# A decoder layer on one core: the third piece of the start moved from SyncE's queue to ScalarE's, and an eighth warming matmul

## The chip, the core and the metric

The kernel runs on one core of a Trainium2 chip. The metric is the device time of one execution in microseconds (us); smaller is better. TensorE (PE) does the matrix products, VectorE (DVE) and ScalarE (ACT) convert operands and evacuate results, GpSimd (POOL) builds masks and loads small parameters, SyncE (SP) issues nearly all transfers. ACT can issue transfers too, on a DMA queue of its own. PE's clock has two levels, 1.2 and 2.4 GHz; the share of the higher one that was granted stands in the profile.

## The reference, cut to what matters

One layer on 256 tokens of width 1024: a SwiGLU channel mixer, a token mixer of three attention branches merged by gates, and a second SwiGLU, each followed by a residual sum and a LayerNorm.

```
D_MODEL, SEQ, D_FF = 1024, 256, 2816

def swiglu(x, w_gate, w_up, w_down):
    return (jax.nn.silu(x @ w_gate) * (x @ w_up)) @ w_down

x = layer_norm(alpha * x + 0.5 * swiglu(x, ffn_w_gate[l, 0], ffn_w_up[l, 0], ffn_w_down[l, 0]), ...)
x = layer_norm(alpha * x + hybrid_mixer(x, w_in[l], ...), ...)
x = layer_norm(alpha * x + 0.5 * swiglu(x, ffn_w_gate[l, 1], ffn_w_up[l, 1], ffn_w_down[l, 1]), ...)
```

Only the first few microseconds of the first `x @ w_gate` and `x @ w_up` matter here. All data are float32.

## The kernel before

Every float32 operand is split into a high part (a copy rounded to the matmul's type, made by ACT or DVE) and a low part (the operand minus its high part, made by DVE). A product is then three matmuls: high times high, low times high, high times low. One helper, `Pe.mm`, records all of them, so that they all stand on line 182.

The contraction over 1024 runs in KT = 8 tiles of 128 rows, called k = 0 to 7. For the start the host lays out an array `start`: for each k a piece of 128 rows by 768 numbers, of which 256 are the transposed activations and 512 are weight columns (the first two column blocks of gate and up). The piece of k is loaded into the tile `sraw{k}` (393,216 bytes, the 384 KB of the trace). SP issues them in order of k on its queue, except that the second half of k = 0 goes on ACT's queue. SP then goes on with the weight chunks `raw<-gu` (line 80) on the same queue.

While these are on the way, PE runs WARM matmuls on a tile of zeros, `warm`, into a bank that is not read. Then, for k = 0, 1, 2, ..., the pieces are split (lines 268 to 277 for k below 3, lines 236 and 237 in the helper `act_split` for the rest), and for each k six matmuls of 512 columns follow: high times high for two halves of the tokens, then activations' low times weights' high, then activations' high times weights' low. The lines are written in order of k for each engine, and each engine works its list in that order. For k = 1 and 2 DVE makes the activations' high part (line 274) and ACT the weights' (line 275). For k from 3 on ACT makes both, activations first.

After the eight k tiles PE goes on to the column blocks 2 to 21 of gate and up, whose weights come as the chunks of line 80, then to the down projection, the mixer and the second SwiGLU. The last work is the LayerNorm of the second half of the tokens and its transfer out.

Of the kernel before, what the change touches and what calls it, by code (L numbers as in the profile page):

```python
# [12 lines left out]
AF = mybir.ActivationFunctionType  # L13
# [19 lines left out]
HL_BUFS = 9  # L33
RAW_BUFS = 5
START = 4
WARM = 7

NAT = 2

# [151 lines left out]
def trunk(ctx: ExitStack, tc: tile.TileContext, start_d, x_d, ln_g, ln_b, gu_d, gun_d, down_d, v_d, qk_d, gate_d,  # L191
          b_gate, lam_d, subln_d, br_d, wo_d, out_d):
    nc = tc.nc
# [41 lines left out]
    def act_split(dst_h, dst_l, src):  # L235
        nc.scalar.activation(dst_h, src, AF.Copy)  # L236
        nc.vector.tensor_tensor(dst_l, src, dst_h.bitcast(F32), op=ALU.subtract)


    with ExitStack() as es:  # L240
        st = es.enter_context(tc.tile_pool(name="start", bufs=1))
        raws = []
        for k in range(KT):
            r = st.tile([P, S + 512], F32, name=f"sraw{k}")
            if k == 0:
                nc.sync.dma_start(out=r[:, 0:384], in_=start_d[k][:, 0:384])  # L246
                nc.scalar.dma_start(out=r[:, 384:768], in_=start_d[k][:, 384:768])
            else:
                nc.sync.dma_start(out=r, in_=start_d[k])  # L249
            raws.append(r)  # L250
        warm = st.tile([P, P], F32, name="warm")
        nc.vector.memset(warm, 0.0)
        wps = att.tile([P, 512], F32, name="att")

        for _ in range(WARM):
            nc.tensor.matmul(wps[:, 0:P], lhsT=warm, rhs=warm, start=True, stop=True)
        ident = const.tile([P, P], F32, name="ident")
        make_identity(nc, ident)
        first = []
        for k in range(KT):  # L260
            if k % 2 == 0:
                w = W.tile(-1 - k)
                first.append(w)
            c = slice((k % 2) * 512, (k % 2) * 512 + 512)
            rx, rw = raws[k][:, 0:S], raws[k][:, S:S + 512]
            if k == 0:

                nc.scalar.activation(xT[:, 0, 0:S], rx, AF.Copy)
                nc.vector.tensor_copy(w[:, 0, 0:P], rw[:, 0:P])
                nc.vector.tensor_copy(w[:, 0, P:512], rw[:, P:512])  # L270
                nc.vector.tensor_tensor(xT[:, 0, S:2 * S], rx, xT[:, 0, 0:S].bitcast(F32), op=ALU.subtract)
                nc.vector.tensor_tensor(w[:, 1, c], rw, w[:, 0, c].bitcast(F32), op=ALU.subtract)
            elif k < 3:
                nc.vector.tensor_copy(xT[:, k, 0:S], rx)
                nc.scalar.activation(w[:, 0, c], rw, AF.Copy)  # L275
                nc.vector.tensor_tensor(xT[:, k, S:2 * S], rx, xT[:, k, 0:S].bitcast(F32), op=ALU.subtract)
                nc.vector.tensor_tensor(w[:, 1, c], rw, w[:, 0, c].bitcast(F32), op=ALU.subtract)
            else:
                act_split(xT[:, k, 0:S], xT[:, k, S:2 * S], rx)
                act_split(w[:, 0, c], w[:, 1, c], rw)  # L280
        W.pump()
# [692 lines left out]
```

## Time and profile before

| | us |
|---|---|
| median of 3 runs | 599.16 (598.97 to 599.27) |
| the profiled execution, its time | 598.51 |
| its span, first to last instruction | 596.8 |
| PE busy in the span | 587.8 |
| DVE busy | 407.5 |
| ACT busy | 328.2 |
| mean granted clock of PE | 0.995 |

The profiled execution's time is its span and 1.71 us around it; it lies 0.65 us under the median of the runs. The busy time of PE is modelled at the ends of matmuls, since they are pipelined: a matmul's end lies behind the start of the next one.

### The profile page before, as it was taken

Reading aid. Unit: us, or ns where it says so; the run is one execution under the profiler, and the core shown is the slowest. Engines: PE = TensorE matmul, PEld = TensorE weight load, DVE = VectorE, ACT = ScalarE, POOL = GpSimd, SP = SyncE. Lnnn points to the kernel's source line nnn. Section 1 sums busy time; section 2 is a strip of 40 time slices with the busy share of each in tenths; the row PEclk is TensorE's granted clock in tenths of the full one; section 3 lists DMA queues with packets and bytes.
Section 4 is the critical chain, followed back from the end, with each engine's and each line's share of the span. In section 5 each row is a group of like instructions: output and inputs, shape, how many; then the busy total and the mean of one; then the engine's idle time right before and its main releaser. Section 6 shows DMA issues by size and latency. Waiting matters only on the chain.

```text
span 596.8 us, 8546 instructions
## 1 busy us (share of the span) xinstructions
PE 587.8 (98%) x3150; PEld 505.2 (85%) x3150; DVE 407.5 (68%) x655; ACT 328.2 (55%) x556; POOL 32.4 (5%) x71
## 2 busy tenths in 40 slices
PE   8999999999999999999999999999999999999995
PEld 7888888888888998888888878888898898888884
DVE  6889767674338746597977685889867667774217
ACT  5868656663312758596657654535665655654100
POOL 1610000000001002110001000001000000000001
PEclk9999999999999999999999999999999999999998
DMA  8999755666431576354547447256965565565001
GB/s 320 316 392 314 241 187 180 207 188 226 141 125 63 200 258 237 118 176 150 171 139 245 145 158 264 97 183 217 330 229 177 180 202 186 180 207 178 1 0 70
DMA packets 32538, 113.34 MB, mean 190 GB/s; under 512 B 3681, under 2 KB 4449, under 8 KB 32497
## 3 DMA queue, kind: packets, MB, share of 16 engines
q1 hardware_dynamic: 30672, 106.77, 53.2%
q0 software_dynamic: 1680, 5.83, 3.0%
q8 instruction: 24, 0.39, 0.3%
q10 hardware_dynamic: 144, 0.20, 0.1%
q14 instruction: 18, 0.14, 0.1%
HBM read 111.74 MB, written 1.05 MB: 189 GB/s over the span
## 4 chain that ended last, share of the span: by engine, by line
PE 97%; DMA 1%; DVE 1%; issue 0%; SPq 0%; ACT 0%; DVEq 0%
PE acc L182 91%; PE att L182 4%; PE att L186 2%; DMA sraw<-start 1%; DVE x L364 0%; DVE x L360 0%; ACT w L275 0%; DVE st L448 0%; DVE x L447 0%; SPq L249 0%; DVEq L968 0%; SPq L246 0%; DVE mv L353 0%
## 5 line engine op out<-in xcount | busy, mean ns | idle before, releaser
L107 DVE TENSOR_TENSOR w<-raw,w 128x1024 fp32r<-128x1024 f32 (+1 forms) x166 | 197.8, 1208 | 61.7 <-ACT w L106 60.8
L182 PE MATMUL acc<-xT,w 128*128 128x512 f32 (+1 forms) x1264 | 226.4, 337 | 0.0
L182 PEld LDWEIGHTS acc<-xT,w 128*128 128x128 f32 x1264 | 196.3, 190 | 26.6 <-issue 1.0
L106 ACT ACTIVATE w<-raw 128x1024 fp32r<-128x1024 f32 (+1 forms) x166 | 170.3, 1042 | 52.2 <-PE acc L182 44.0
L182 PE MATMUL acc<-w,xT 128*128 128x512 f32 (+1 forms) x576 | 128.1, 379 | 0.0
L182 PEld LDWEIGHTS acc<-w,xT 128*128 128x128 f32 x576 | 105.5, 188 | 18.6 <-issue 1.0
L182 PE MATMUL acc<-w,hT 128*128 128x512 f32 (+1 forms) x408 | 93.1, 383 | 0.0
L182 PEld LDWEIGHTS acc<-w,hT 128*128 128x128 f32 x408 | 75.2, 188 | 14.9
L475 ACT ACTIVATE lo<-acc 128x256 f32<-128x256 f32 x76 | 28.8, 384 | 57.3 <-PE acc L182 57.3
L477 DVE TENSOR_TENSOR gu<-acc,lo 128x256 f32<-128x256 f32 x76 | 31.6, 423 | 34.7 <-ACT lo L475 34.6
L182 PE MATMUL acc<-xT,wx 128*128 128x256 f32 (+1 forms) x240 | 46.1, 337 | 0.0
L107 DVE TENSOR_TENSOR wx<-raw,wx 128x1024 fp32r<-128x1024 f32 (+1 forms) x30 | 36.3, 1214 | 12.5 <-ACT wx L106 12.5
L182 PEld LDWEIGHTS acc<-xT,wx 128*128 128x128 f32 x240 | 37.5, 190 | 4.4
L106 ACT ACTIVATE wx<-raw 128x1024 fp32r<-128x1024 f32 (+1 forms) x30 | 31.3, 1047 | 11.3 <-PE acc L182 10.2
L354 ACT ACTIVATE rs<-mv 128x1 f32<-128x1 f32 x6 | 1.2, 204 | 59.6 <-DVE mv L353 59.6
L182 PE MATMUL acc<-wx,hT 128*128 128x512 f32 (+1 forms) x138 | 32.8, 380 | 0.0
L182 PEld LDWEIGHTS acc<-wx,hT 128*128 128x128 f32 x138 | 25.2, 188 | 4.9
L355 POOL TENSOR_TENSOR rs<-rs,mhalf 128x1 f32<-128x1 f32 x6 | 5.3, 892 | 407.9 <-ACT rs L354 407.9
L346 DVE SCALAR_TENSOR_TENSOR x<-x,acc 128x512 f32<-128x512 f32 x11 | 7.5, 683 | 27.4 <-PE acc L182 27.4
L182 PE MATMUL acc<-w,oT 128*128 128x512 f32 x108 | 25.7, 393 | 0.0
L182 PEld LDWEIGHTS acc<-w,oT 128*128 128x128 f32 x108 | 20.1, 188 | 4.4 <-issue 0.3
L236 ACT ACTIVATE hT<-gu 128x256 fp32r<-128x256 f32 x38 | 15.8, 417 | 11.5 <-DVE gu L482 11.5
(146 smaller groups left out, 412.9 us busy)
## 6 DMA issues: line engine op xcount, KB each, us to landing
raw<-gu SPq DMA_DIRECT2D x76, 512.0 KB, 4.8
raw<-down SPq DMA_DIRECT2D x44, 512.0 KB, 4.2
raw<-gates SPq DMA_DIRECT2D x24, 512.0 KB, 4.4
raw<-qk SPq DMA_DIRECT2D x18, 512.0 KB, 4.5
raw<-v SPq DMA_DIRECT2D x12, 384.0 KB, 3.0
raw<-w_out SPq DMA_DIRECT2D x8, 512.0 KB, 4.3
raw<-gun SPq DMA_DIRECT2D x8, 512.0 KB, 4.3
sraw<-start SPq DMA_DIRECT2D x7, 384.0 KB, 6.6
```

Of the source, the lines that this page charges most:

```text
L106: self.nc.scalar.activation(h[:, :n], raw[:, :n], AF.Copy)
L107: self.nc.vector.tensor_tensor(l[:, :n], raw[:, :n], hv[:, :n], op=ALU.subtract)
L182: self.nc.tensor.matmul(out, lhsT=lhsT, rhs=rhs, start=start, stop=stop, **kw)
L186: self.nc.tensor.transpose(out, in_, ident)
L236: nc.scalar.activation(dst_h, src, AF.Copy)
L346: nc.vector.scalar_tensor_tensor(xs, xs, ALPHA, ps[:, 0:n], op0=ALU.mult, op1=ALU.add)
L354: nc.scalar.activation(rs, mv[:, 1:2], AF.Copy, bias=EPS)
L355: nc.gpsimd.tensor_tensor(rs, rs, mhalf[:, 0:1], op=ALU.pow)
L475: nc.scalar.activation(lo, ps[:, S:2 * S], AF.Copy)
L477: nc.vector.tensor_tensor(v, ps[:, 0:S], lo, op=ALU.add)
```

## The change

The third piece, k = 2, is no longer issued by SP between the pieces of k = 1 and 3. ACT issues it, on its own queue. Ahead of that transfer ACT runs an activation of one column from `warm` into the piece's own tile; since the transfer writes the same tile, it waits for that activation, and the activation needs ACT's function table, so the table is loaded first. And there are eight warming matmuls in place of seven.

```
-WARM = 7
+WARM = 8
...
             if k == 0:
                 nc.sync.dma_start(out=r[:, 0:384], in_=start_d[k][:, 0:384])
                 nc.scalar.dma_start(out=r[:, 384:768], in_=start_d[k][:, 384:768])
-            else:
+            elif k != 2:
                 nc.sync.dma_start(out=r, in_=start_d[k])
             raws.append(r)
         warm = st.tile([P, P], F32, name="warm")
         nc.vector.memset(warm, 0.0)
+
+
+        nc.scalar.activation(raws[2][:, 0:1], warm[:, 0:1], AF.Copy)
+        nc.scalar.dma_start(out=raws[2], in_=start_d[2])
```

ACT's list from the program's beginning, before the change (the number behind a name tells buffers apart; what a row waits for stands in brackets, DMAHW for transfers):

```order
L247 DMA sraw0_90<-start 128x384
L268 ACT_TABLE_LOAD
L268 ACTIVATE xT_86<-sraw0_90 128x256 [waits DMAHW1_49]
L275 ACTIVATE w_122<-sraw1_93 128x512 [waits DMAHW2_49]
L275 ACTIVATE w_132<-sraw2_95 128x512 [waits DMAHW3_49]
L236 ACTIVATE xT_86<-sraw3_97 128x256 [waits DMAHW4_49]
```

The same place after the change, where the lines below the edit have numbers higher by 4:

```order
L247 DMA sraw0_90<-start 128x384
L255 ACT_TABLE_LOAD
L255 ACTIVATE sraw2_95<-warm_106 128x1 [waits DVE_49]
L256 DMA sraw2_95<-start 128x768 [waits Activation_49]
L272 ACTIVATE xT_86<-sraw0_90 128x256 [waits DMAHW1_49]
L279 ACTIVATE w_124<-sraw1_93 128x512 [waits DMAHW2_49]
L279 ACTIVATE w_134<-sraw2_95 128x512 [waits DMAHW4_49]
L236 ACTIVATE xT_86<-sraw3_96 128x256 [waits DMAHW3_49]
```

The table load keeps its place; one activation and one transfer have come in between it and the first conversion of k = 0, and the conversion of k = 2 still stands ahead of those of k = 3.

SP's list from the beginning, before:

```order
L246 DMA sraw0_90<-start 128x384
L249 DMA sraw1_93<-start 128x768
L249 DMA sraw2_95<-start 128x768
L249 DMA sraw3_97<-start 128x768
L249 DMA sraw4_99<-start 128x768
```

And after:

```order
L246 DMA sraw0_90<-start 128x384
L249 DMA sraw1_93<-start 128x768
L249 DMA sraw3_96<-start 128x768
L249 DMA sraw4_98<-start 128x768
L249 DMA sraw5_100<-start 128x768
```

The piece of k = 3 now follows that of k = 1 directly, and each later transfer of SP has moved up by one place.

## Rows read from the trace of the kernel before

**Rows 1.** The page: busy time of each engine, then the chain that ended last

```profile
PE 587.8 (98%) x3150; PEld 505.2 (85%) x3150; DVE 407.5 (68%) x655; ACT 328.2 (55%) x556; POOL 32.4 (5%) x71
...
PE 97%; DMA 1%; DVE 1%; issue 0%; SPq 0%; ACT 0%; DVEq 0%
```

**Rows 2.** PE's waits, whole span: in total, times, longest, us

```profile
PE att L256 <- DVE warm L252: 1.1, 1, 1.1
PE att L182 <- ACT w L275: 0.6, 1, 0.6
```

**Rows 3.** Chain that ended last, us 0 to 40: start, length, what

```profile
1.23 0.42 SPq L249
1.65 0.05 issue
1.70 5.57 DMA sraw<-start
7.26 0.02 issue
7.29 0.64 ACT w L275
7.92 0.04 issue
7.97 8.47 PE att L182 x36
```

**Rows 4.** PE in order of time, us 0 to 22: start, length, line, count

```profile
1.10 3.36 PE L256 MATMUL att<-warm 128*128 128x128 f32 x14 [1.10 <-DVE warm L252]
4.35 3.02 PE L182 MATMUL att<-w,xT 128*128 128x512 f32 x12
7.97 8.47 PE L182 MATMUL att<-w,xT 128*128 128x512 f32 x36 [0.60 <-ACT w L275]
16.27 5.10 PE L182 MATMUL acc<-xT,w 128*128 128x512 f32 x27
21.21 0.27 PE L186 MATMUL att<-ident,gu 128*128 128x128 f32 x1
21.32 0.27 PE L186 MATMUL att<-ident,hid 128*128 128x128 f32 x1
```

**Rows 5.** Groups of instructions in us 0 to 16.2: count, busy, mean ns

```profile
L182 PE MATMUL att<-w,xT 128*128 128x512 f32 x48 | 11.5, 395 | 0.6 <-ACT w L275 0.6
```

**Rows 6.** ACT in order of time, us 0 to 22

```profile
1.22 1.28 ACT L268 ACT_TABLE_LOAD   x1 [1.22 <-PEq L964]
3.67 0.42 ACT L268 ACTIVATE xT<-sraw 128x256 fp32r<-128x256 f32 x1 [1.17 <-DMA sraw<-start]
4.80 0.63 ACT L275 ACTIVATE w<-sraw 128x512 fp32r<-128x512 f32 x1 [0.71 <-DMA sraw<-start]
...
8.27 0.42 ACT L236 ACTIVATE xT<-sraw 128x256 fp32r<-128x256 f32 x1 [0.35 <-DMA sraw<-start]
8.59 0.62 ACT L236 ACTIVATE w<-sraw 128x512 fp32r<-128x512 f32 x1
```

**Rows 7.** SP's first transfers in order of time: start, length, count

```profile
1.23 3.48 SPq L249 DMA_DIRECT2D sraw<-start  x7
```

**Rows 8.** Issue to landing (last number, us): k = 1, 2, 3, from three stretches

```profile
sraw<-start SPq DMA_DIRECT2D x1, 384.0 KB, 3.5
...
sraw<-start SPq DMA_DIRECT2D x1, 384.0 KB, 5.6
...
sraw<-start SPq DMA_DIRECT2D x1, 384.0 KB, 6.1
```

**Rows 9.** Four stretches: length, busy by engine, PE's clock, DMA share, GB/s

```profile
0.00:4.00 4.00, 2.90 (x13) 2.90 (x14) 0.49 (x3) 1.61 (x2) 0.75 (x7) 1.00 0.55 176
4.00:7.00 3.00, 3.00 (x15) 2.31 (x13) 2.38 (x6) 0.72 (x2) 0.00 (x0) 1.00 0.89 262
4.50:6.50 2.00, 2.00 (x9) 1.59 (x10) 1.88 (x5) 0.63 (x1) 0.00 (x0) 1.00 0.76 204
7.00:9.00 2.00, 1.40 (x6) 0.86 (x5) 1.60 (x4) 1.36 (x3) 0.00 (x0) 1.00 1.03 410
```

**Rows 10.** DMA queues in us 2.5 to 3 (q1 SP's, q10 ACT's): packets

```profile
q1 hardware_dynamic: 59, 0.09, 51.6%
q10 hardware_dynamic: 59, 0.09, 48.7%
```

**Rows 11.** The page: a small activation, and a transfer of the same size

```profile
L354 ACT ACTIVATE rs<-mv 128x1 f32<-128x1 f32 x6 | 1.2, 204 | 59.6 <-DVE mv L353 59.6
...
raw<-v SPq DMA_DIRECT2D x12, 384.0 KB, 3.0
```

**Rows 12.** Two stretches after PE's last matmul, columns as in group 9

```profile
590.00:591.00 1.00, 0.00 (x0) 0.00 (x0) 0.92 (x3) 0.20 (x1) 0.00 (x0) 1.00 0.00 0
591.00:592.00 1.00, 0.00 (x0) 0.00 (x0) 1.00 (x2) 0.00 (x0) 0.88 (x1) 0.71 0.00 0
```

## The prediction

> **What bounds the kernel now.** I read the page first: PE is busy in 98% of the span, and the chain that ended last is PE for 97% [rows 1]. So I looked for the places where PE waits. There are two in the whole span [rows 2]: 1.1 us at the very beginning, for the zeros of the warming matmuls, and 0.6 us at line 182 for ACT's conversion at line 275. Everything PE does after that second wait follows without another, so what the start gains or loses arrives at the end one for one.
>
> The chain through the first microseconds shows what that wait is [rows 3]. A transfer of a start piece, issued by SP, landed at 7.26; ACT converted the weights of the piece from 7.29 for 0.64 us; PE began at 7.97, with 36 matmuls, which are six k tiles of six. Two k tiles (12 matmuls) ran before it [rows 4]. So the piece is that of k = 2. The distance from landing to PE is 7.97 - 7.26 = 0.71 us.
>
> How long is the hole really? From 7.97 to the next group at 16.27 the 36 matmuls start 8.30 / 36 = 0.231 us apart [rows 4], while one lasts 0.395 us with its modelled end [rows 5]. After the 12th, whose modelled end is 4.35 + 3.02 = 7.37, the next could have started at 7.37 - 0.395 + 0.231 = 7.21. The hole is 7.97 - 7.21 = 0.76 us. That is the most that an earlier k = 2 could give back.
>
> Why did k = 2 land late? From issue to landing k = 1 took 3.5 us, k = 2 5.6, k = 3 6.1 [rows 8]. The issues follow each other by about 0.48 us (seven from 1.23 in 3.48 us [rows 7], and the chain's first at 1.23), so k = 1 landed at about 4.8 (its conversion starts at 4.80 [rows 6]), k = 2 at 7.26 and k = 3 at about 8.25 (its conversion starts at 8.27 [rows 6]). Between k = 1 and k = 2 lie 2.5 us; from 7 to 9 us the engines move 410 GB/s, at which a piece of 393,216 bytes takes 0.96 us. The difference is a dip: from 4.5 to 6.5 us only 204 GB/s move [rows 9]. In it the DMA engines were 0.76 busy, against 1.03 at full rate [rows 9]. At full efficiency 204 GB/s would need 1.03 x 204 / 410 = 0.51. So of the half that is lost, about half (0.76 - 0.51) is transfers that took longer and half (1 - 0.76) is engines with nothing to move, although SP had issued five pieces by then. What starves them no view shows.
>
> **The change part by part.** The base of the sum is the profiled execution, 598.51 us, which lies 0.65 under the median of 599.16. I carry the difference over.
>
> *ACT's two new instructions.* The table load stands where it stood, from 1.22 to 2.50 [rows 6]. An activation of one column costs about 0.20 [rows 11], and the transfer's issue about 0.45 (an issue of the same size on SP [rows 7]). ACT is free at about 3.2. Its next work, the conversion of k = 0, started at 3.67 after 1.17 us of idling for a transfer [rows 6]. So they cost nothing; the cover that is left is 0.5 us.
>
> *SP's list.* One issue fewer; everything behind k = 1 is issued 0.45 us earlier. That gains nothing by itself, since the transfers take 0.96 us each and the issues 0.48: the queue is ahead anyway. It matters only in that k = 3 now stands behind k = 1 directly.
>
> *The eighth warming matmul.* It is two records of the group x14. These started about (3.36 - 0.4) / 13 = 0.23 us apart (0.4 stands for the last one's own length, near the 0.395 of [rows 5]), while records of the same shape at line 186 start 0.11 apart [rows 4]: the warm-up runs at the lower level of the clock, 1.2 GHz, though the clock's column reads 1.00 there as well [rows 9]; the k tiles run at the higher one, 2.4 GHz, from their start. Two records cost 0.46 at the lower level, 0.22 at the higher. The rise lies right about here, so I take 0.25, with 0.2 to 0.45 as the bounds. Then the k tiles 0 and 1 end at 7.21 + 0.25 = 7.46. That is still ahead of 7.97, so the hole covers the whole cost as long as k = 2 arrives later than 7.46 - 0.71 = 6.75. Where it arrives sooner, the cover is gone, and the gain ends at 0.76 - 0.25 = 0.51.
>
> *When k = 2 now lands.* This is the term that decides. It is issued at about 2.50 + 0.20 + 0.05 = 2.75 in place of 1.70. A lone transfer of the same size takes 3.0 us from issue to landing [rows 11], which gives 5.75 as the lowest bound. But it isn't alone. Where both queues had work, they shared the engines packet by packet: 59 packets each in half a microsecond [rows 10]. With a first packet some 1.2 us after issue (the halves of k = 0 were issued at 0.79 and shared by 2.5), k = 2 starts near 4.0, when k = 1 is nearly through, and then alternates with k = 3. So it ends shortly ahead of k = 3, with two or three of k = 3's eight packets per engine left: 0.10 to 0.15 MB, or 0.24 to 0.36 us; I take 0.3.
>
> When do k = 0 to 3 have all their bytes? They are 4 x 0.393 = 1.573 MB. By 4.0 us 0.704 MB had moved, by 7.0 another 0.787 [rows 9]; the last 0.08 at 410 GB/s end at 7.2. From the last byte to the landing of the slowest engine k = 1 took about 0.5 us (its bytes, 0.786 MB with k = 0, are through near 4.3), k = 3 about 1.05 (8.25 - 7.2). Three outcomes:
> - The dip stays as it is: k = 2 has its bytes at 7.2 - 0.3 = 6.9 and lands at 7.4 to 7.95, later than the 7.26 of before. PE starts it at 8.1 to 8.65: a loss of 0.14 to 0.69.
> - The idle half of the dip is filled, since a second queue gives an engine something to move when the first has nothing ready: the dip cost 2 us x (410 - 204) GB/s = 0.41 MB, or 1.0 us; half of it is 0.5. k = 2 has its bytes at 6.4 and lands at 6.9 to 7.2 (with a lag of 0.5 to 0.8, shorter since the dip is). Against 7.26 that is 0.05 to 0.35 sooner; I take 0.2.
> - The dip vanishes: k = 2 has its bytes at 5.9, lands at 6.4 and PE no longer waits: 0.51 gained.
>
> I take the middle one: the idle share is there in the rows, and a queue with work can use it. The sum is 598.51 + 0 (ACT) + 0 (SP) + 0 (warming, covered) - 0.2 = 598.3; carried to the median, **598.95**.
>
> **The rivals.**
> 1. *Sharing makes k = 2 later* (the dip stays as it is). For it: 59 against 59 packets, an issue a whole microsecond later, and SP's issue time never bound. Against it: the idle 0.24 of the dip. Then 599.16 + 0.14 to 0.69 = 599.3 to 599.85. The Trainium skill, page "DMA: Bandwidth & Descriptors", section "Issuing engines are not separate DMA queues", says that transfers started by different engines run on the same 16 DMA engines and interleave, and that issuing from several saves only the sequencer's time. By that rule this rival is the outcome; the trace agrees on the interleaving, and no row tells whether a second queue fills holes.
> 2. *k = 3 becomes the wait.* ACT takes k = 2 before k = 3, and k = 3's weights are ready at 8.59 + 0.62 = 9.21, about 9.25 with the hop to PE. PE came to it at 7.97 + 6 x 0.231 = 9.36 at the earliest. If k = 2 comes early and k = 3 stays at 8.25, the gain stops at 0.1 to 0.2: 598.95 to 599.05. For it: the bytes of k = 0 to 3 are the same in sum. Against it: k = 3 is issued 0.45 sooner, and a filled dip brings it along.
> 3. *The clock falls* (the other side). PE's hole starts at 7.46. At the program's end the last matmul ended at about 589.5 and the granted clock was still 1.00 until 591 and 0.71 in the next microsecond [rows 12], so it was halved some 1.8 us after PE fell idle, while the hole of 0.76 us left it at 1.00 [rows 9]. If k = 2 landed after 7.46 + 1.8 - 0.71 = 8.55, PE would begin at 9.26 or later, a loss of 1.3, and would start at 1.2 GHz: each k tile takes 6 x 0.231 = 1.4 us at the higher level and so 1.4 more at half of it. With one tile at the lower level: 599.16 + 1.3 + 1.4 or more = 601.9 and up. For it: a transfer on ACT's queue that comes behind all of k = 3 and k = 4. Against it: the fair sharing.
>
> **How the numbers follow.** The forecast (k = 2 lands 6.4 to 7.2, gain 0.05 to 0.51) has 0.52. Rival 1 has 0.30, rival 2 0.12, rival 3 0.04; 0.02 is for a gain that I see no way to. The range 598.4 to 599.9 takes in the forecast with all its bounds (599.16 - 0.51 = 598.65, and 0.25 for the scatter of a median, half of the 598.97 to 599.27 and more) and rivals 1 and 2; rival 3 stays out. A difference under 0.2%, 1.2 us, is about what a measurement of this kernel can't tell from none. No case but rival 3 and the unseen gain passes it: faster 0.02, slower 0.05 (rival 3 and a little of rival 1's upper end), within 0.93.
>
> **What the changed profile would show.** Eight warming matmuls as x16 records, with the first k tile starting at 4.55 to 4.8. An ACT issue at about 2.75, and packets of ACT's queue from about 4.0, as many as SP's. The conversion of k = 2's weights at about 7.05 in place of 7.29, and PE's hole shrunk from 0.76 to under 0.35. A DMA rate from 4.5 to 6.5 us clearly over 204 GB/s, at a busy share nearer 1. The conversion of k = 3 right behind, by 7.8 or so. From there every group of PE earlier by the same 0.2.
>
> What would make it wrong: a k = 2 that lands after 7.26 (rival 1), a PE wait at line 182 for line 236 (rival 2), a granted clock that falls between 7 and 12 us (rival 3), or a rise of the clock that the eighth matmul moves.

## The result, and the profile after

The changed kernel takes 601.9 us (median of 6 executions, 600.98 to 603.0), the kernel before 599.07 (6 executions, 597.87 to 599.28). The measured ratio is 1.0052, with a 95% interval of 1.004 to 1.0063 (the two medians alone give 1.0047): slower by half a per cent. The forecast was 598.95, with 599.9 as its upper end.

The page of the changed kernel, as in [rows 1]: busy times, then the chain.

```profile
PE 589.5 (98%) x3152; PEld 506.4 (84%) x3152; DVE 406.6 (68%) x655; ACT 327.0 (54%) x557; POOL 33.4 (6%) x71
...
PE 97%; DMA 1%; DVE 1%; ACT 0%; issue 0%; ACTq 0%; DVEq 0%
```

Shares of the span tell nothing here. PE's waits, to be read against [rows 2], do:

```profile
PE att L182 <- ACT w L279: 3.1, 1, 3.1
```

It is the same wait on the same conversion (line 279 is line 275 of before), now 3.1 us and not 0.6. The chain that ended last in the first 40 us, the counterpart of [rows 3] (start, length, what):

```profile
2.52 0.21 ACT sraw L255
2.73 0.02 issue
2.75 7.05 DMA sraw<-start
9.80 0.02 issue
9.82 0.64 ACT w L279
10.46 0.04 issue
10.51 10.07 PE att L182 x36
```

ACT issues k = 2 at 2.75, as planned, but the piece lands at 9.80, where before it landed at 7.26. From landing to PE it is 0.71 us, as before. PE in order of time, us 0 to 23 (with [rows 4]):

```profile
4.45 2.99 PE L182 MATMUL att<-w,xT 128*128 128x512 f32 x12
10.51 10.07 PE L182 MATMUL att<-w,xT 128*128 128x512 f32 x36 [3.07 <-ACT w L279]
20.42 2.88 PE L182 MATMUL acc<-xT,w 128*128 128x512 f32 x12
```

Two things are lost. PE restarts at 10.51, not 7.97: 2.54 us. And the same 36 matmuls take 20.42 - 10.51 = 9.91 us to the next group in place of 8.30: 1.61 us. Together 4.15, and the profiled execution is 602.65 - 598.51 = 4.14 us longer. The second loss is the clock's. Three stretches (columns as in [rows 9]), and the matmuls of the second of them (minimum, median and maximum length, ns):

```profile
9.00:10.50 1.50, 0.00 (x0) 0.00 (x0) 0.64 (x3) 0.68 (x2) 0.00 (x0) 1.00 1.03 416
10.80:14.10 3.30, 3.30 (x9) 2.52 (x9) 3.30 (x8) 3.30 (x9) 0.00 (x0) 0.50 1.02 415
14.20:16.00 1.80, 1.80 (x9) 1.46 (x9) 1.80 (x5) 1.80 (x3) 0.00 (x0) 1.00 1.01 405
...
L182 PE MATMUL att<-w,xT x9: 533/628/628, 10.5 to 13.9; 128*128 128x512 f32 x9
```

PE idles from about 7.4 to 10.5. The granted clock still reads 1.00 at the end of this hole; it is 0.50 (1.2 GHz) from 10.8 to 14.1, with PE already back at work, then 1.00 again. Nine matmuls ran in 3.3 us there, 0.628 us long, and nine in 1.8 us behind it. Not every execution pays this. It shows best in the spans: two of the six have 600.8 and 600.9 us, at a mean granted clock of 0.995; the other four have 598.9 to 599.5, near 596.8 + 2.54 = 599.3, which is the hole alone. The slowest time, 603.0, belongs to the shortest of these spans, 598.9: what it has more lies outside the span and is no loss of PE's. The median of 601.9 lies between the two groups.

Where did k = 2 stay so long? First the distance from issue to landing (last number, us) of k = 1, 3, 4 and 5 from SP, each from its own stretch, and of k = 2 from ACT:

```profile
sraw<-start SPq DMA_DIRECT2D x1, 384.0 KB, 3.7
...
sraw<-start SPq DMA_DIRECT2D x1, 384.0 KB, 5.0
...
sraw<-start SPq DMA_DIRECT2D x1, 384.0 KB, 6.2
...
sraw<-start SPq DMA_DIRECT2D x1, 384.0 KB, 7.0
sraw<-start ACTq DMA_DIRECT2D x1, 384.0 KB, 7.1
```

SP's issues lie 0.47 apart from 1.23 on, at 1.23, 1.70, 2.17 and 2.64, and ACT's at 2.75. So the landings are about 4.9, 6.7, 8.4, 9.6 and 9.8: the order of issue over both queues. Then the packets by queue (q1 SP's, q10 ACT's), in us 3.6 to 5.9 and in us 6.7 to 7.7:

```profile
q1 hardware_dynamic: 269, 0.73, 103.7%
...
q1 hardware_dynamic: 68, 0.18, 50.7%
q10 hardware_dynamic: 61, 0.19, 47.2%
```

In the first stretch SP's packets fill the DMA engines (103.7% of their time) and ACT's queue has none, although its transfer was issued at 2.75. Only later do the two alternate. The first packets of k = 2 fall into us 5.9 to 6.4:

```profile
q1 hardware_dynamic: 44, 0.13, 74.3%
q10 hardware_dynamic: 7, 0.02, 10.6%
```

That is over 3.1 us after the issue.

### The profile page after: what moved, and what is told of

Its sections match the earlier page's. It is cut to its first block, busy times and chain, and to the rows that moved or that the text cites. A ratio compares the mean times of both kernels' runs of the same rounds, so it can differ in the third digit from the quotient of the medians.

```text
span 600.9 us, 8551 instructions
## 1 busy us (share of the span) xinstructions
PE 589.5 (98%) x3152; PEld 506.4 (84%) x3152; DVE 406.6 (68%) x655; ACT 327.0 (54%) x557; POOL 33.4 (6%) x71
## 4 chain that ended last, share of the span: by engine, by line
PE 97%; DMA 1%; DVE 1%; ACT 0%; issue 0%; ACTq 0%; DVEq 0%
PE acc L182 91%; PE att L182 5%; PE att L186 2%; DMA sraw<-start 1%; ACT L255 0%; DVE x L368 0%; DVE x L364 0%; ACT w L279 0%; DVE st L452 0%; DVE x L451 0%; ACTq L247 0%; DVEq L972 0%; DVE mv L357 0%; ACT sraw L255 0%
## 5 line engine op out<-in xcount | busy, mean ns | idle before, releaser
L106 ACT ACTIVATE wx<-raw 128x1024 fp32r<-128x1024 f32 (+1 forms) x30 | 31.3, 1046 | 10.8 <-PE acc L182 10.2
```

Source lines behind the costliest of these rows:

```text
L106: self.nc.scalar.activation(h[:, :n], raw[:, :n], AF.Copy)
```

## The experiments

Theories: **A**, a transfer gets under way by its place among all issues, both queues taken together, so k = 2 is late because it is issued fifth. **B**, ACT's queue is itself served badly beside SP's. **C**, the eighth warming matmul upsets the clock. **A1** and **A2**, named below, refine A.

| kernel | median, us | ratio to before (95% interval) | k = 2's conversion starts |
|---|---|---|---|
| before | 598.73 to 599.07, by comparison | 1 | 7.29 |
| changed | 601.9 | 1.0052 (1.004 to 1.0063) | 9.82 |
| eighth warming matmul alone | 599.0 | 1.0005 (0.9996 to 1.0015) | 7.62 |
| move to ACT alone | 601.37 | 1.0052 (1.0037 to 1.0067) | 9.82 |
| ACT issues k = 2 early | 598.52 | 0.9997 (0.9988 to 1.0007) | right behind k = 1's, 5.77 |
| SP issues k = 2 fifth | 602.29 | 1.0065 (1.0042 to 1.0088) | 10.11 |
| changed, SP held from k = 4 | 599.07 | 1.0005 (0.9996 to 1.0015) | 7.69 |
| changed, SP held from k = 5 | 600.53 | 1.0033 (1.0023 to 1.0042) | 9.40 |
| changed, PE kept busy | 601.26 | 1.0038 (1.0024 to 1.0051) | 9.72 |
| before, SP held from k = 3 | 598.91 | 1.0 (0.999 to 1.001) | 6.16 |
| k = 1 and 2 in halves | 598.72 | 1.0002 (0.9993 to 1.0011) | 8.23 |
| GpSimd issues k = 2 | 599.88, one execution | none | 7.86 |

**The two parts of the change.** Before, with `WARM = 8`:

> The eighth warming matmul alone; k = 2 stays on SP's queue. Theory A (the transfer of k = 2 is late because it is issued late, behind k = 3 to 5): time within 0.4 us of the kernel before, k = 2's conversion near 7.3, PE's hole about 0.5. Theory C (the eighth matmul upsets the clock): 1.5 us or more slower, with a fall of the granted clock between 7 and 15 us.

And the changed kernel with `WARM = 7`:

> The move to ACT's queue alone, with seven warming matmuls. Theory A: as the changed kernel, 1.5 to 4 us slower than before, k = 2's conversion between 9 and 10.5. Theory C: within 0.5 us of the kernel before.

The eighth matmul alone measures as no change; the move alone gives the loss, with the conversion again at 9.82 and, in the profiled execution, the clock again at 0.50 afterwards. C falls.

**The place among the issues.** ACT issues k = 2 early, on the same queue:

```
+            elif k == 2:
+                nc.scalar.dma_start(out=r, in_=start_d[k])
             else:
                 nc.sync.dma_start(out=r, in_=start_d[k])
```

> k = 2 on ACT's queue, but issued right behind ACT's half of k = 0 at about 1.2, ahead of the table load and without the small activation; seven warming matmuls. Theory A (the place among all issues decides): k = 1 and k = 2 share the engines and both land at 5.5 to 6.5, time within 0.5 us of the kernel before, possibly 0.3 faster. Theory B (ACT's queue is served badly beside a full SP queue): k = 2 lands after 8.5, 1.5 us or more slower.

And SP issues it late, with no second queue:

```
-            else:
+            elif k != 2:
                 nc.sync.dma_start(out=r, in_=start_d[k])
             raws.append(r)
+            if k == 5:
+                nc.sync.dma_start(out=raws[2], in_=start_d[2])
```

> One queue only: SP issues k = 2 behind k = 5, at about 3.1, ACT nothing but its half of k = 0; seven warming matmuls. Theory A: k = 2 lands as the fifth piece, at 9.5 to 10.3, PE idles about 3 us and the time is 2 to 4 us over the kernel before, much as the changed kernel. Theory B says nothing against that, but holds ACT's queue itself at fault, so that the fifth place on SP's queue would be better than the changed kernel by 0.5 us or more.

With ACT's issue at 1.23 beside SP's of k = 1, the queues share from the beginning. Packets in us 3.5 to 5 of that run:

```profile
q1 hardware_dynamic: 104, 0.30, 50.1%
q10 hardware_dynamic: 98, 0.30, 49.0%
```

PE doesn't wait at line 182 at all there, and the time is that of before. (Both pieces land later than k = 1 did before, and PE's first matmuls ran slow in this execution, up to 0.767 us; that it would not wait otherwise isn't shown.) With the fifth place on SP's own queue, ACT's order of time shows the same late conversion as in the changed kernel:

```profile
10.11 0.63 ACT L277 ACTIVATE w<-sraw 128x512 fp32r<-128x512 f32 x1 [4.62 <-DMA sraw<-start]
```

So ACT's queue did no harm when it got a whole piece early, and SP's does the same harm when used late. B falls in this plain form and A stands, with an open end that the halves show below.

**How many issues stand ahead.** To take SP's later issues away without a bare wait, GpSimd copies one column of k = 1's piece into the tile of k = 4 (or 5), which the transfer overwrites; SP must then wait until k = 1 has landed.

```
             elif k != 2:
+                if k == 4:
+                    nc.gpsimd.tensor_copy(r[:, 0:1], raws[1][:, 0:1])
                 nc.sync.dma_start(out=r, in_=start_d[k])
```

> The changed kernel, but SP issues k = 4 and all behind it only when k = 1 has landed (GpSimd copies a column of k = 1's piece into k = 4's tile, which the transfer then overwrites), at about 5.2. So when ACT issues k = 2 at 2.75, only k = 1 and k = 3 stand ahead. Theory A1 (transfers of both queues get under way in the order of issue): the first packets of ACT's queue come at 4 to 5 and k = 2 is converted at 6 to 7, PE's hole shrinks to under 0.8, time within 0.6 us of the kernel before. Theory A2 (nothing new gets under way on any queue until about 6 us, whatever stands ahead): ACT's first packets stay at 6 or later, k = 2 is converted after 7.8, 0.8 us or more slower than before.

And with `k == 5`:

> The changed kernel with SP held from k = 5 on (until k = 1 has landed), so that k = 4 is the one further transfer that stands ahead of ACT's k = 2. Theory A1: k = 2 converted between the 7.7 of the hold from k = 4 and the 9.8 of no hold, at 8.2 to 9.2; PE's hole 1 to 2 us, time 0.7 to 2 us over the kernel before. Theory A2 (a matter of time, not of what stands ahead): as the hold from k = 4, converted before 8, within 0.5 us of before; or as no hold, converted after 9.5.

The packets. Held from k = 4, in us 3.6 to 4.9 and in us 5.2 to 6.2:

```profile
q1 hardware_dynamic: 116, 0.31, 84.5%
...
q10 hardware_dynamic: 73, 0.22, 57.0%
q1 hardware_dynamic: 72, 0.18, 45.9%
```

Held from k = 5, in us 3.6 to 5.9 and in us 6.1 to 7:

```profile
q1 hardware_dynamic: 278, 0.76, 94.5%
...
q10 hardware_dynamic: 71, 0.22, 67.7%
q1 hardware_dynamic: 47, 0.11, 31.9%
```

With one piece behind k = 1 ahead of it, ACT's packets are missing until 4.9; with two, until 5.9, as with three in the changed kernel. The conversions, in the same order:

```profile
7.69 0.63 ACT L281 ACTIVATE w<-sraw 128x512 fp32r<-128x512 f32 x1 [1.52 <-DMA sraw<-start]
```

```profile
9.40 0.63 ACT L281 ACTIVATE w<-sraw 128x512 fp32r<-128x512 f32 x1 [4.03 <-DMA sraw<-start]
```

Issue to landing says it once more: held from k = 4, k = 3 lands at 1.70 + 5.7 = 7.4 and k = 2 at 2.75 + 4.9 = 7.65; held from k = 5, k = 4 lands at 2.17 + 7.0 = 9.2 and k = 2 at 2.76 + 6.6 = 9.4. In both, as in the changed kernel, k = 2 lands 0.2 us behind the last piece issued ahead of it. But the sizes missed. Held from k = 4, the conversion was expected at 6 to 7 and came at 7.69, close to the 7.8 that A2 named, and ACT's first packets were expected at 4 to 5 and came about 5; the time is that of before, as A1 said. Held from k = 5, 9.40 is 0.2 over A1's bound and 0.1 under A2's 9.5, PE waited 2.7 us where 1 to 2 were expected, and ACT's packets start no earlier than without a hold. So the landing goes with the number ahead (7.65, 9.4 and 9.8 with one, two and three pieces), but the first packets differ only between one and two, so that A2 isn't wholly out. Nor is it shown that only pieces issued ahead count: each hold also delays those that SP issues behind 2.75, and no run holds these alone.

**The clock's share.** The changed kernel, with PE busy through the hole:

```
+                    if k == 1:
+                        for _ in range(13):
+                            nc.tensor.matmul(wps, lhsT=xT[:, 0, 0:P], rhs=w[:, 0, 0:512], start=True, stop=True)
```

> The changed kernel with 13 more matmuls behind those of k = 1 (k = 0's operands, 512 columns, into the bank that is not read), so that PE is busy during its wait for k = 2. If the second part of the loss is the clock's fall: PE's groups start where they do in the changed kernel (about 10.5), the six k tiles after it take 8.3 to 8.5 us in place of 9.9, no granted clock under 1 between 8 and 20 us, and every execution lies near the lower group of the changed kernel, 600.8 to 601.2. If the clock is not at work: as the changed kernel, spread from 601.0 to 603.0.

```profile
7.60 3.11 PE L501 MATMUL att<-w,xT 128*128 128x512 f32 x13
10.55 8.32 PE L182 MATMUL att<-w,xT 128*128 128x512 f32 x36
```

The data is as late as in the changed kernel (10.55), but the 36 matmuls take 8.32 us with their modelled end where the changed kernel's took 10.07. The granted clock reads 1.00 from 10.6 to 18. Three of the five executions lie at 600.89 to 601.26, about as stated, and two at 601.8 and 601.88, above it for a reason that isn't known. The first loss, the late piece, stays. That the second is the clock's fall rests on the changed kernel's own rows, a granted 0.50 and matmuls of 0.628 us; this run agrees. That a busy PE prevents the fall is likely but not shown by five times, since four of the six executions of the changed kernel don't have it either. (The profiled executions of the changed kernel, of the move alone, of SP's late issue and of the hold from k = 5 all have it.)

**Can the hole of before be won?** SP of the kernel before, held from k = 3 until its half of k = 0 has landed:

```
             else:
+                if k == 3:
+                    nc.gpsimd.tensor_copy(r[:, 0:1], raws[0][:, 0:1])
                 nc.sync.dma_start(out=r, in_=start_d[k])
```

> The kernel before, but SP issues k = 3 and all behind it only when its half of k = 0 has landed, at about 4.1. If the dip of the DMA rate between 4.5 and 6.5 comes from the many transfers issued ahead: no dip, k = 2 converted at 5.7 to 6.2, no hole of PE, 0.4 to 0.8 us faster than before. If the dip comes whatever is issued (a matter of time): rate stays near 200 GB/s, k = 2 converted near 7.3, time within 0.3 us of before.

The rate from 4.5 to 6.5 us rose (352 GB/s, before 204) and fell later (264 from 7 to 9), k = 2 was converted at 6.16 and PE never waited at line 182. Yet the time is that of before, against the 0.4 to 0.8 us expected. PE's matmuls of the start from 4.4 to 7 us, in the profiled execution and in that of the kernel before, give a reason (minimum, median and maximum, ns):

```profile
L182 PE MATMUL att<-w,xT x6: 503/628/764, 4.4 to 6.7; 128*128 128x512 f32 x6
...
L182 PE MATMUL att<-w,xT x12: 387/396/467, 4.3 to 7.0; 128*128 128x512 f32 x12
```

0.628 us is the length at 1.2 GHz, as in the stretch at a granted 0.50 of the changed kernel (the clock's column reads 1.00 here, as it does in the warm-up). In this execution the clock rose late, and PE itself was slow where it no longer waited. In the kernel before, the hole would hide such a late rise. Whether all ten executions rose late no trace tells.

The halves of k = 1 and 2 issued by SP and ACT at once (`if k < 3` in place of `if k == 0`), and k = 2 issued by GpSimd:

> The pieces of k = 1 and 2 are issued in halves, by SP and ACT at the same time, as that of k = 0 is in all kernels; the order of the pieces stays k = 0, 1, 2, 3 on both queues, ACT issues before its table load, seven warming matmuls. Theory A1 (order of issue over both queues decides, and two queues in use leave no dip): k = 1 converted by 5.0, k = 2 by 6.0 to 6.6, no wait of PE at line 182. The time gains at most the hole of 0.76; where PE's clock rises late (after 5 us, seen in several profiles), the k tiles 0 and 1 take longer and less or nothing is gained: 0 to 0.7 us faster than before. If ACT's queue is at fault by itself: k = 1 and k = 2 land later than in the kernel before, and the time is 0.5 us or more over it.

> k = 2 issued by GpSimd on its queue at the program's start (about 0.8 to 1.8), seven warming matmuls, no small activation. If any second queue served early will do (theory A): k = 1 and k = 2 share and land at 5.5 to 6.5, no dip, PE's hole under 0.7, span within 1 us of the kernel before. If only ACT's queue does it: k = 2 converted after 7.3.

Both missed on the landing. In halves, k = 1 was converted at 5.10 but k = 2 only at 8.23, and 285 GB/s moved from 4.5 to 6.5: two queues in use do not by themselves remove the dip. From issue to landing, k = 3 from SP (issued at 2.17) and the two halves of k = 2 (both issued at 1.70):

```profile
sraw<-start SPq DMA_DIRECT2D x1, 384.0 KB, 6.2
sraw<-start SPq DMA_DIRECT2D x1, 192.0 KB, 5.2
sraw<-start ACTq DMA_DIRECT2D x1, 192.0 KB, 6.5
```

ACT's half landed at 8.2, 1.3 us behind SP's half issued at the same moment and only 0.2 ahead of k = 3, issued 0.47 later. The order of issue doesn't give that. Both pieces landed later than in the kernel before, the sign that was named for a fault of ACT's queue itself, though the time didn't rise by the 0.5 us that went with it. So a weaker form of B, a queue that falls behind a full one, stays open. On GpSimd's queue the conversion came at 7.86, outside what A gave; with one execution this only says that an early issue there is no gain. No version tried beats the kernel before by more than its measurement can tell.

## Why the prediction was wrong

*What bounds the kernel*: right. The hole of PE at line 182, the 0.71 us from landing to PE and the path of every microsecond to the end held to 0.01 us (2.54 + 1.61 against 4.14). A slip without effect: by the dip SP had issued not five pieces but all seven.

*ACT's instructions*: right. The activation took 0.20, the issue started at 2.75 and took 0.34, and k = 0's conversion came at 3.76. *The eighth matmul*: PE's first k tile starts at 4.45 after 4.35, 0.1 in place of 0.25 (4.54, or 0.19, with the eighth matmul alone), and the hole covers it.

*SP's list* was read by its issue times alone: "That gains nothing by itself". True for SP, but the step past it did the harm: with k = 2 taken out and issued at 2.75, k = 3, 4 and 5 were issued ahead of it.

*When k = 2 now lands* is the step that failed: "With a first packet some 1.2 us after issue", so that "k = 2 starts near 4.0, when k = 1 is nearly through, and then alternates with k = 3". The 1.2 us came from the halves of k = 0, the first issues of the program, and the sharing from [rows 10], 59 packets against 59. Those rows show how two queues share once both have packets, not when the packets of a transfer begin that is issued a microsecond after others. The runs show the latter: nothing of k = 2 until 5.9, over 3.1 us after its issue, and a landing at 9.80 where the three outcomes named 6.4, 6.9 to 7.2 and 7.4 to 7.95. The alternation itself came, from then on.

*The dip* that the middle outcome would fill: 283 GB/s moved from 4.5 to 6.5 at a busy share of 1.00, the sign that was named. But ACT's queue had no packet there until 5.9, and the eighth matmul alone, with the transfers of before, shows 272 GB/s against the 204 of before. So the rate here tells nothing of the second queue.

*Rival 1* rested on the same early start and was too small for the same reason, 0.14 to 0.69 against 2.54. The Trainium skill, page "DMA: Bandwidth & Descriptors", section "Issuing engines are not separate DMA queues", says that transfers of different engines interleave and that a second issuing engine saves only issue time. The trace agrees on the interleaving once both queues have packets (68 against 61, and 73 against 72 under the hold from k = 4), and no early issue on a second queue gained time here (ratio 0.9997 for ACT's). When the later transfer's packets begin, the measurement decides.

*Rival 2* didn't come to be as a wait of its own: k = 3 landed at 6.7, well before k = 2, and stood behind it on ACT's list until 10.36.

*Rival 3* is what happened, down to its condition, "a transfer on ACT's queue that comes behind all of k = 3 and k = 4", and a landing after 8.55. Its price, 601.9 and up, is the measured median, but by luck, for the parts came out otherwise: PE at 10.51 rather than 9.26, 1.61 for the clock rather than 1.4, and the clock in two executions of six only. Nor did the clock fall 1.8 us after PE fell idle, as read from [rows 12]: it still read 1.00 at 10.5, 3 us into the hole. Its chance of 0.04 was the error, taken from the fair sharing. The price of a late place stood in the trace of before, where [rows 8] stops at k = 3. From issue to landing of k = 4 and k = 5, the fourth and fifth whole pieces, before:

```profile
sraw<-start SPq DMA_DIRECT2D x1, 384.0 KB, 6.6
...
sraw<-start SPq DMA_DIRECT2D x1, 384.0 KB, 7.1
```

The fifth place took 7.1 us on SP's queue, and k = 2 in the fifth place on ACT's took 7.05.

## What to carry to other kernels

Before moving a transfer to another queue, list all issues of all queues by time and count what stands ahead of it at its new time. In the changed kernel and under both holds it landed 0.2 us behind the last transfer issued before it, on the other queue; the halves, where ACT's lagged 1.3 us behind SP's of the same moment, show that even this can be too hopeful. A row in which two queues alternate tells how they share, not when a later transfer begins. And a hole of PE has two prices, the wait and, here with a hole of 3 us and in two executions of six, the clock behind it.

## What was not expected of the hardware

A second queue gave no way past transfers issued earlier on the first: ACT's packets came from about 5 with one piece ahead beyond k = 1, from about 6 with two and with three. What delays them (the making of descriptors or their fetching) no view shows; it stays open. So does the dip of the DMA rate around 5 us, one profile each: 204 GB/s before, 272 with the same transfers and an eighth warming matmul, 283 in the changed kernel, 285 in halves, 352 with the kernel before and SP held, and none when ACT issued k = 2 at 1.23. The first two differ by 68 with nothing changed in the transfers, so differences of this size tell nothing. The one without a dip:

```profile
4.50:6.50 2.00, 2.00 (x6) 1.60 (x7) 1.44 (x5) 0.73 (x2) 0.00 (x0) 1.00 1.02 403
```

The clock's rise at the start differs from execution to execution: the median matmul from 4.4 to 7 us lasts 0.396 us in the profile of before and 0.628 in that of the kernel before with SP held, with the same seven warming matmuls ahead. In the five profiles with eight it is 0.389 to 0.397; whether the eighth matmul helps there, these few don't tell, and its time alone shows no gain.
